# A WKV recurrence in chunks: numerators in two PSUM banks, state matmuls in the banks of the denominators, sums in 256 columns, v converted on the chip

## The chip, the cores and the metric

The kernel runs on one core of a Trainium2 chip. The metric is the time of one execution on the device, in microseconds (us). A core has five engines with in-order queues: PE (matmuls, with its weight loads shown apart as PEld), DVE (elementwise work), ACT (exponentials and logarithms), POOL and SP (here mostly issuers of DMAs). Matmul results go to PSUM, which has eight banks of 512 float32 columns in 128 partitions; everything else lives in SBUF. Transfers between device memory and SBUF are DMAs.

## What is computed

For each of 16 batches and 256 channels a recurrence runs over 2048 time steps. Without the running maximum `pp`, which only keeps the exponentials in range, it is a decayed sum of `exp(k)*v` over a decayed sum of `exp(k)`, with an extra weight `u` on the present step:

```python
for b in range(batch):                 # 16
    aa = bb = zeros(256); pp = full(256, -1e38)
    for t in range(seq_len):           # 2048
        kk, vv = k[b, t], v[b, t]
        ww = u + kk
        qq = maximum(pp, ww)
        e1, e2 = exp(pp - qq), exp(ww - qq)
        output[b, t] = (e1 * aa + e2 * vv) / (e1 * bb + e2 + 1e-08)
        ww = pp - w + kk
        qq = maximum(ww, kk)
        e1, e2 = exp(ww - qq), exp(kk - qq)
        aa, bb, pp = e1 * aa + e2 * vv, e1 * bb + e2, qq
```

k, v and the output are 33.6 MB each in float32.

## The kernel before

Time is cut into 16 chunks of 128 steps (two halves of 64), and the 16 batches into four groups of four. One pair of chunk c and group p is a slot, n = 4c + p, so there are 64 slots. A slot's tile has the 128 steps on the partitions and 4 batches x 256 channels = 1024 columns. A chunk is four slots.

In a slot n the main loop (L342) issues, for several slots at once:

- `load` (L62): the DMAs of k and v of slot n+6, on POOL's queue. For n of 8 and more and odd, `v_mode` (L59) says "dma", and the DMA converts v to bf16 on its way (`vb`, L70); otherwise v arrives as float32 (`vr`, L74) and DVE converts it (`cast_v`, L191).
- `round_k` (L161, DVE): k of slot n+2 is copied to a tile `km` in the matmul's float32 format.
- `logs` (L164, PE): eight matmuls make the exponents X of slot n+1 (decays from w and u, L170; k itself, L174) in four PSUM banks.
- `exps` (L178, ACT): exp of X of slot n, 2048 columns, into planes 0 and 1 of the ring EZR, which holds 12 slots. `times_v` (L196, DVE) multiplies them by v into planes 2 and 3.
- `den` (L296, PE): the denominators of slot q = n-9: four matmuls over planes 0 and 1 into two PSUM banks. `recip` (L302, L303, ACT): their reciprocals, by a logarithm and an exponential.
- `num` (L309, PE): half a numerator of slot qp = n-10: two matmuls over planes 2 and 3 into one PSUM bank. `mult` (L316, DVE): that half times the reciprocal, into the output tile. Both run twice a slot, and since there is one bank, the second `num` starts after the first `mult`. `store` (L321): the output's DMA, on POOL's queue.

The state at the end of a chunk has to reach all later chunks, and this is small work spread over the slots after the chunk's last one, s = 4c + 3:

- `sums` (L213, PE, slot s+1): 16 matmuls with 32 output rows, four beside each other in the array, sum the planes 0 and 2 of four slots over time, into one bank `tot` of 512 columns. `copy_sums` (L225, DVE) copies it to SBUF (`ts`).
- `turn` (L232, PE, s+2): matmuls that put the channels on the partitions (`TS`). `state_logs` (L237, ACT), `state_offsets` (L243 to L250, DVE): logarithms of the sums and the running offsets.
- `state_weights` (L254, ACT, s+3), `state_chain` (L261 to L268, DVE): the state itself; it reads TS again.
- `turn_back` (L275, PE, s+4): matmuls back to time order (`CT`). `inject` (L280, DVE): a copy to `cb`, and then four DMAs on SP's queue (L285) which patch one row of each half in the ring slots of the same chunk c with the state that enters it, before `den` (from slot 4c+9 on) and `num` read them.

`tot`, `TS` and `CT` share one PSUM bank of their own (pool `psm`). So the eight banks are X four, den two, num one, state work one. Every instruction keeps the order in which the program issues it on its engine (`K`). The list `later` (L324) says at which point of a slot a piece of state work is issued: "pe0", "act" and "dve0" come right after `exps`, before `num` and `den`; "pe" and "dve" come at the slot's end. So PE meets `turn` and `turn_back` at the head of a slot, before num and den of that slot.

The prediction names the lines of this kernel.

Of the kernel before, what the change touches and what calls it, by code (L numbers as in the profile page):

```python
# [7 lines left out]
F32 = mybir.dt.float32  # L8
F32R = mybir.dt.float32r
BF16 = mybir.dt.bfloat16  # L10
ALU = mybir.AluOpType
ACT = mybir.ActivationFunctionType
# [3 lines left out]
def kernel(  # L16
# [9 lines left out]
    K = tc.keep_in_program_order  # L26
    PE, DVE, SC, POOL, SP = nc.tensor, nc.vector, nc.scalar, nc.gpsimd, nc.sync

    B, T, Dm = k.shape
    HS = 64  # L30
# [18 lines left out]
    psx = ctx.enter_context(tc.tile_pool(name="psx", bufs=1, space=bass.MemoryType.PSUM))  # L49
    psd = ctx.enter_context(tc.tile_pool(name="psd", bufs=1, space=bass.MemoryType.PSUM))  # L50
    psn = ctx.enter_context(tc.tile_pool(name="psn", bufs=1, space=bass.MemoryType.PSUM))
    psm = ctx.enter_context(tc.tile_pool(name="psm", bufs=1, space=bass.MemoryType.PSUM))

    K(SC.preload_act_table_set("natural_log_exp_and_others"))

# [1 line left out]
    kr_of, vr_of, VB = {}, {}, {}  # L57

    def v_mode(n):  # L59
        return "dve" if n < 8 or n % 2 == 0 else "dma"  # L60

    def load(n, kq=None, vq=None):  # L62
        c, p = divmod(n, 4)
# [29 lines left out]
    def select(ap, cmp, fill, base, cm, pattern):  # L93
        K(POOL.affine_select(out=ap, in_=ap, pattern=pattern, compare_op=cmp,
                             fill=fill, base=base, channel_multiplier=cm))
# [4 lines left out]
    def fill(ap, value):  # L100
        K(DVE.memset(ap.bitcast(F32) if ap.dtype == F32R else ap, value))
# [1 line left out]
    select(M1, GE, 0.0, -1, -1, [[1, 128]])  # L103
    select(I1, NE, 1.0, 0, -1, [[1, 128]])
    COf = matrix("COf", F32)
    for h in range(2):
        K(POOL.iota(COf[HS * h:HS * h + HS, :], pattern=[[0, 2], [1, HS]], base=-HS // 2 - h, channel_multiplier=0,
                    allow_small_or_imprecise_dtypes=True))
    for g in (2, 3):
        select(COf, NE, 1.0, -32 * g - 1, 1, [[0, 128]])  # L110
# [15 lines left out]
    mats = {}  # L126

    def sum_matrices():
        OH = consts.tile([128, 40], BF16, tag="OH", name="OH")
        fill(OH, 0.0)  # L130
        for h in range(2):
            fill(OH[HS * h:HS * h + HS, 8 + h:9 + h], 1.0)
            fill(OH[HS * h:HS * h + 1, 16 + h:17 + h], 1.0)
        Sel = consts.tile([128, 3, 2, 4, 2], F32, tag="Sel", name="Sel")
        fill(Sel, 0.0)
        for j, r in ((0, 64), (1, 0), (2, 8)):
            select(Sel[:, j], NE, 1.0, -r, 1, [[-1, 2], [-2, 4], [-32, 2]])
        mats["OH"], mats["Sel"] = OH, Sel.rearrange("p a h c i -> p (a h) (c i)")

    def out_matrices():  # L140
        Lx = matrix("Lx", F32)
# [14 lines left out]
    def ez(n):  # L156
        return EZR[:, :, n % RING]

    def round_k(n):
        km = consts.tile([128, 4, Dm], F32R, tag=f"km{n % 2}", name="km") if n < 2 else KM[n - 2]  # L160
        K(DVE.tensor_copy(km, kr_of.pop(n)))  # L161
        KM[n] = km
# [37 lines left out]
    LL = consts.tile([128, 2, 2 * NST + 2, 32], F32, tag="LL", name="LL")  # L200
    A_of = [consts.tile([128, 8, 32], F32, tag=f"A{j}", name=f"A{j}") for j in range(2)]
    AB_of = [consts.tile([128, 2, 2, 32], F32, tag=f"AB{j}", name=f"AB{j}") for j in range(2)]

    CB_of = [consts.tile([128, 4, 128], BF16, tag=f"CB{j}", name=f"CB{j}") for j in range(2)]

    def state_start():
# [4 lines left out]
        K(DVE.memset(AB_of[0][:, :, 0, :], 0.0))  # L211

    def sums(c):  # L213
        t = psm.tile([128, D], F32, tag="misc", name="tot")
        for p in range(4):
            for j in range(4):
                q, i = divmod(j, 2)
                K(PE.matmul(t[32 * j:32 * j + 32, :], mats["OH"][:, 8 - 2 * p:40 - 2 * p],  # L218
                            ez(4 * c + p)[:, 2 * q, i, :], start=p == 0, stop=p == 3,
                            tile_position=(0, 32 * j), skip_group_check=True))  # L220
        st[c, "tot"] = t

    def copy_sums(c):
        ts = tiny.tile([128, D], F32, tag="ts", name="ts")
        K(DVE.tensor_copy(ts, st.pop((c, "tot"))))  # L225
        st[c, "ts"] = ts

    def turn(c):
        TS = psm.tile([128, 6, 4, 8], F32, tag="misc", name="TS")
        ts = st.pop((c, "ts"))  # L230
        for b in range(4):
            K(PE.matmul(TS[:, :, b, :], ts[:, 128 * b:128 * b + 128], mats["Sel"], start=True, stop=True,  # L232
                        skip_group_check=True))
        st[c, "TS"] = TS.rearrange("p a b m -> p a (b m)")

    def state_logs(c):
        K(SC.activation(LL[:, :, 2 * c + 2:2 * c + 4, :],  # L237
                        st[c, "TS"][:, 2:6, :].rearrange("p (a h) x -> p a h x", a=2), ACT.Ln))

    def state_offsets(c):  # L240
        A, last = A_of[c % 2], A_of[(c + 1) % 2]
# [13 lines left out]
        st[c, "G"] = G  # L255

    def state_chain(c):
        G, TS = st.pop((c, "G")), st.pop((c, "TS"))
        AB, nxt = AB_of[c % 2], AB_of[(c + 1) % 2]
        tb = tiny.tile([128, 2, 2, 32], F32, tag="tb", name="tb")  # L260
        K(DVE.tensor_mul(tb, TS[:, 0:4, :].rearrange("p (a h) x -> p a h x", a=2),  # L261
                         G[:, 4:6, :].unsqueeze(1).broadcast_to([128, 2, 2, 32])))
        for h in range(2):
            x = tiny.tile([128, 2, 32], F32, tag="x", name="x")
            K(DVE.tensor_mul(x, AB[:, :, h, :], G[:, h, :].unsqueeze(1).broadcast_to([128, 2, 32])))
            K(DVE.tensor_add(AB[:, :, 1, :] if h == 0 else nxt[:, :, 0, :], x, tb[:, :, h, :]))
        CB = CB_of[c % 2]
        K(DVE.tensor_mul(bass.AP(tensor=CB.tensor, offset=CB.offset, ap=[list(CB.ap[0]), [64, 2], [32, 2], [129, 4], [4, 8]]),  # L268
                         AB.rearrange("p a h (b m) -> p a h b m", b=4),
                         G[:, 2:4, :].rearrange("p h (b m) -> p h b m", b=4).unsqueeze(1).broadcast_to([128, 2, 2, 4, 8])))  # L270

    def turn_back(c):
        CT = psm.tile([128, 128], F32, tag="misc", name="CT")
        for b in range(4):
            K(PE.matmul(CT, CB_of[c % 2][:, b, :], mats["Id"], start=b == 0, stop=b == 3, skip_group_check=True))  # L275
        st[c, "CT"] = CT

    def inject(c):
        cb = small.tile([128, 128], BF16, tag="cb", name="cb")
        K(DVE.tensor_copy(cb, st.pop((c, "CT"))))  # L280
        r0 = 4 * c % RING
        for q in range(2):
            for h in range(2):
                r, x = HS * h + HS - 1, 32 * (2 * q + h)
                K(SP.dma_start(  # L285
                    out=EZR[r:r + 1, 2 * (1 - q), r0:r0 + 4, :, :].rearrange("o p i (b x) -> o (p i b) x", b=4),
                    in_=cb[x:x + 32, :]))
# [15 lines left out]
        K(SC.activation(rd, rd, ACT.Exp, scale=-1.0))  # L303
        RD[n] = rd

    def num(n, i):
        d = psn.tile([128, D], F32, tag="num", name="num")
        for m, q in (("LN", 2), ("IdN", 3)):
            K(PE.matmul(d, mats[m], ez(n)[:, q, i, :], start=q == 2, stop=q == 3, skip_group_check=True))  # L309
        NUM[n, i] = d  # L310

    def mult(n, i):
        if i == 0:
            OT[n] = opool.tile([128, 4, Dm], F32, tag="ot", name="ot")
        o = OT[n].rearrange("p (i n) d -> p i (n d)", i=2)
        K(DVE.tensor_mul(o[:, i, :], NUM.pop((n, i)), RD[n][:, i, :]))  # L316

    def store(n):
        RD.pop(n)
        c, p = divmod(n, 4)  # L320
        K(POOL.dma_start(out=out[4 * p:4 * p + 4, c * TC:(c + 1) * TC, :].rearrange("n t d -> t n d"),  # L321
                         in_=OT.pop(n)))

    later = {}  # L324
    for c in range(NST):
        s = 4 * c + 3
        for slot, where, f in ((s + 1, "pe", sums), (s + 1, "dve", copy_sums),
                               (s + 2, "pe0", turn), (s + 2, "act", state_logs), (s + 2, "dve", state_offsets),
                               (s + 3, "act", state_weights), (s + 3, "dve", state_chain),
                               (s + 4, "pe0", turn_back), (s + 4, "dve0", inject)):  # L330
            later.setdefault((slot, where), []).append((f, c))

    def small_work(n, where):
        for f, c in later.pop((n, where), []):
            f(c)
# [6 lines left out]
    for n in range(NP + LAG + 2):  # L342
        q, qp = n - LAG, n - LAG - 1
        live, out_q, out_qp = n < NP, 0 <= q < NP, 0 <= qp < NP
        if n + AHEAD < NP:
            load(n + AHEAD)
        if live:
            exps(n)
        small_work(n, "pe0")
        small_work(n, "act")  # L350
        small_work(n, "dve0")
        if out_qp:
            num(qp, 0)
        if out_q:
            den(q)
            recip(q)
        if out_qp:
            mult(qp, 0)
            num(qp, 1)
        if n + 1 < NP:  # L360
            logs(n + 1)
        if n + 2 < NP:
            round_k(n + 2)
        if out_qp:
            mult(qp, 1)
            store(qp)
        if live:
            times_v(n)
        if n + 1 < NP:
            cast_v(n + 1)  # L370
        if n == 1:
            sum_matrices()
        if n == 3:
            out_matrices()
        small_work(n, "pe")
        small_work(n, "dve")
    assert not later


# [29 lines left out]
```

## Time and profile before

| | |
|---|---|
| runs | 403.47, 408.91, 400.68 us; median 403.47 |
| profiled execution | 401.16 us, of which the recorded span is 399.2 |
| mean granted clock of PE in it | 0.923 of full |
| ACT: L178, L302, L303 | 64 each, mean 1875, 1019, 1061 ns |
| DVE: L196, L316 (512 columns), L161, L191 | 64, 128, 64, 36 of 1216, 690, 688, 698 ns |
| PE: L174, L296, L309 | 256, 254, 235 records |
| DMA from POOL's queue | 37824 packets, 91.24 MB, 78.2% of 16 engines' span |
| POOL issues: stores, k, v, v converted | 64, 62, 34, 28 |

The profiled execution is one run of the program on the chip with every instruction recorded. An engine's busy time is the sum of its instructions; idle time is put down to what released the instruction after it. A matmul's recorded end is modelled, and matmuls overlap, so their starts say more than their lengths. Some matmul records are missing (235 of 256 for L309).

### The profile page before, as it was taken

Reading aid. Unit: us, or ns where it says so; the run is one execution under the profiler, and the core shown is the slowest. Engines: PE = TensorE matmul, PEld = TensorE weight load, DVE = VectorE, ACT = ScalarE, POOL = GpSimd, SP = SyncE. Lnnn points to the kernel's source line nnn. Section 1 sums busy time; section 2 is a strip of 40 time slices with the busy share of each in tenths; the row PEclk is TensorE's granted clock in tenths of the full one; section 3 lists DMA queues with packets and bytes.
Section 4 is the critical chain, followed back from the end, with each engine's and each line's share of the span. In section 5 each row is a group of like instructions: output and inputs, shape, how many; then the busy total and the mean of one; then the engine's idle time right before and its main releaser. Section 6 shows DMA issues by size and latency. Waiting matters only on the chain.

```text
span 399.2 us, 4440 instructions
## 1 busy us (share of the span) xinstructions
PE 286.8 (72%) x1449; PEld 133.9 (34%) x1472; DVE 283.7 (71%) x559; ACT 260.6 (65%) x225; POOL 158.9 (40%) x203
## 2 busy tenths in 40 slices
PE   0345769787868697777789686869777778957672
PEld 0122334343424334333334242433433333423220
DVE  1266665877787877878777878787787977776542
ACT  1134344975777877877758777777787775876472
POOL 7134322452545453535435454545353531012131
PEclk9999857996999889999969999988999996999896
DMA  7978975699899989999989899997999991333344
GB/s 245 349 248 193 316 202 136 174 284 257 264 254 296 273 204 282 261 279 281 287 237 287 264 295 250 302 275 208 280 262 286 268 285 56 105 109 138 122 165 158
DMA packets 43062, 94.15 MB, mean 236 GB/s; under 512 B 6160, under 2 KB 22560, under 8 KB 43040
## 3 DMA queue, kind: packets, MB, share of 16 engines
q0 software_dynamic: 37824, 91.24, 78.2%
q1 hardware_dynamic: 4144, 1.59, 1.7%
q10 hardware_dynamic: 1072, 1.06, 0.9%
q8 instruction: 11, 0.18, 0.2%
q14 instruction: 11, 0.09, 0.1%
HBM read 67.13 MB, written 33.55 MB: 252 GB/s over the span
## 4 chain that ended last, share of the span: by engine, by line
PE 34%; DVE 29%; issue 21%; DMA 7%; ACT 4%; POOL 3%; POOLq 0%; DVEq 0%
DVE EZR L196 10%; PE num L309 10%; PE X L174 7%; DVE ot L316 7%; PE den L296 6%; DMA kr<-in_k_dram 4%; PE tot L218 3%; ACT EZR L178 3%; PE TS L232 3%; POOL out_dram L321 3%; DVE vb L191 3%; PE X L170 3%; DVE ts L225 2%; DMA out_dram<-ot 1%; DMA vr<-in_v_dram 1%
## 5 line engine op out<-in xcount | busy, mean ns | idle before, releaser
L178 ACT ACTIVATE EZR<-X 128x2048 bf16<-128x2048 f32 x64 | 120.0, 1875 | 51.7 <-PE X L174 51.4
L321 POOL DMA_DIRECT2D out_dram<-ot x64 | 48.9, 763 | 196.5 <-DVE ot L316 192.6
L316 DVE TENSOR_TENSOR ot<-num,rd 128x512 f32<-128x512 f32 x128 | 88.3, 690 | 53.7 <-PE num L309 44.5
L302 ACT ACTIVATE rd<-den 128x1024 f32<-128x1024 f32 x64 | 65.2, 1019 | 51.3 <-PE den L296 51.3
L196 DVE TENSOR_TENSOR EZR<-EZR,vb 128x2048 bf16<-128x2048 bf16 x64 | 77.8, 1216 | 5.4 <-ACT EZR L178 5.3
L309 PE MATMUL num<-EZR,LN 128*128 128x512 bf16 x121 | 49.0, 405 | 35.2 <-DVE ot L316 34.6
L303 ACT ACTIVATE rd<-rd 128x1024 f32<-128x1024 f32 x64 | 67.9, 1061 | 2.0
L66 POOL DMA_DIRECT2D kr<-in_k_dram x62 | 55.7, 899 | 16.9 <-DVE km L161 14.8
L170 PE MATMUL X<-WU,CO 1*128 1x512 f32 (+1 forms) x256 | 36.1, 554 | 27.9 <-ACT EZR L178 15.1
L174 PE MATMUL X<-km,NLE 128*128 128x512 f32 x128 | 51.9, 489 | 3.3 <-DVE km L161 3.3
L161 DVE CAST km<-kr 128x1024 fp32r<-128x1024 f32 x64 | 44.0, 688 | 8.6 <-DMA kr<-in_k_dram 6.1
L309 PE MATMUL num<-EZR,IdN 128*128 128x512 bf16 x114 | 46.3, 406 | 0.4
L174 PE MATMUL X<-km,NLZ 128*128 128x512 f32 x128 | 45.5, 440 | 0.0
L296 PE MATMUL den<-EZR,Id 128*128 128x512 bf16 x128 | 40.9, 403 | 0.1
L296 PE MATMUL den<-EZR,L 128*128 128x512 bf16 x126 | 40.4, 403 | 0.7
L170 PEld LDWEIGHTS X<-WU,CO 1*128 1x128 f32 (+1 forms) x256 | 13.5, 202 | 58.3 <-ACT EZR L178 26.5
L74 POOL DMA_DIRECT2D vr<-in_v_dram x34 | 31.0, 912 | 2.4 <-DVE vb L191 2.4
L309 PEld LDWEIGHTS <-IdN 128*128 128x128 bf16 x128 | 13.1, 102 | 54.7 <-issue 54.7
L174 PEld LDWEIGHTS X<-km,NLZ 128*128 128x128 f32 x128 | 27.0, 211 | 6.9
L174 PEld LDWEIGHTS X<-km,NLE 128*128 128x128 f32 x128 | 21.0, 207 | 21.5 <-issue 17.2
L232 PE MATMUL TS<-Sel,ts 128*128 128x48 f32 x128 | 17.4, 279 | 12.9 <-DVE ts L225 12.9
L275 PE MATMUL CT<-Id,CB 128*128 128x128 bf16 x64 | 7.6, 254 | 25.8 <-DVE CB L268 25.8
(53 smaller groups left out, 214.2 us busy)
## 6 DMA issues: line engine op xcount, KB each, us to landing
out_dram<-ot POOLq DMA_DIRECT2D x64, 512.0 KB, 4.1
kr<-in_k_dram POOLq DMA_DIRECT2D x62, 512.0 KB, 6.2
vr<-in_v_dram POOLq DMA_DIRECT2D x34, 512.0 KB, 6.6
vb<-in_v_dram POOLq DMA_DIRECT2D x28, 256.0 KB, 7.2
kr<-in_k_dram SPq DMA_DIRECT2D x2, 512.0 KB, 14.3
vr<-in_v_dram ACTq DMA_DIRECT2D x2, 512.0 KB, 5.7
EZR<-cb SPq DMA_DIRECT2D x64, 8.0 KB, 4.8
wuf<-in_w_dram SPq DMA_DIRECT2D x4, 2.0 KB
```

The lines of the kernel that those rows point to most:

```text
L66: K((kq or POOL).dma_start(out=kr, in_=src[0]))
L161: K(DVE.tensor_copy(km, kr_of.pop(n)))
L170: K(PE.matmul(X[:, q, i, :], CO[g:g + 1 + q, :], WU[g:g + 1 + q, :], start=True, stop=False, tile_position=(g, 0), skip_group_check=True))
L174: K(PE.matmul(X[:, q, i, :], m, km[:, i, :], start=False, stop=True, skip_group_check=True))
L178: K(SC.activation(ez(n)[:, 0:2], X_of.pop(n), ACT.Exp))
L196: K(DVE.tensor_mul(ez(n)[:, 2:4], ez(n)[:, 0:2], vb.unsqueeze(1).broadcast_to([128, 2, 2, D])))
L296: K(PE.matmul(d[:, i, :], mats[m], ez(n)[:, q, i, :], start=q == 0, stop=q == 1, skip_group_check=True))
L302: K(SC.activation(rd, DEN.pop(n), ACT.Ln, scale=RS))
L303: K(SC.activation(rd, rd, ACT.Exp, scale=-1.0))
L309: K(PE.matmul(d, mats[m], ez(n)[:, q, i, :], start=q == 2, stop=q == 3, skip_group_check=True))
L316: K(DVE.tensor_mul(o[:, i, :], NUM.pop((n, i)), RD[n][:, i, :]))
L321: K(POOL.dma_start(out=out[4 * p:4 * p + 4, c * TC:(c + 1) * TC, :].rearrange("n t d -> t n d"), in_=OT.pop(n)))
```

## The change

Six things are edited together.

1. `num` and `mult` work on a whole slot: four matmuls into two PSUM banks, and one DVE multiply of 1024 columns instead of two of 512.
2. The bank that this takes comes from state work: the pool `psm` is gone, and `tot`, `TS` and `CT` are allocated from `den`'s pool, which has one buffer. So they and the denominators follow one another in the same two banks.
3. `sums` writes 256 columns instead of 512: 32 matmuls of 256 columns, with the matrix OH shifted by 16 rows for the second half; the copy is half as wide, and `turn` takes two matmuls instead of four (with a wider Sel).
4. A new copy `copy_turned` (DVE) takes the 192 turned columns out of PSUM, and `state_logs` and `state_chain` read the copy.
5. `v_mode` always says "dve": no DMA converts, and DVE converts all of v.
6. The order: state work on PE comes last in its slot, behind `logs`, and its copies come last on DVE (a new point, "last"). `state_logs`, `state_offsets` and `state_weights` move to slot s+3 (the weights behind `recip`, "act2"), `state_chain` to the head of s+4 on DVE, with its small products in a new order, `turn_back` and `inject` to the end of s+4. `cast_v` comes before `mult`, and `times_v` after it.

```diff
     def v_mode(n):
-        return "dve" if n < 8 or n % 2 == 0 else "dma"
+        return "dve"
...
     def sums(c):
-        t = psm.tile([128, D], F32, tag="misc", name="tot")
+        t = psd.tile([128, 2, D], F32, tag="den", name="tot")
         for p in range(4):
-            for j in range(4):
-                q, i = divmod(j, 2)
-                K(PE.matmul(t[32 * j:32 * j + 32, :], mats["OH"][:, 8 - 2 * p:40 - 2 * p],
-                            ez(4 * c + p)[:, 2 * q, i, :], start=p == 0, stop=p == 3,
-                            tile_position=(0, 32 * j), skip_group_check=True))
+            for o in range(2):
+                x = 24 - 16 * o - 2 * p
+                for j in range(4):
+                    q, i = divmod(j, 2)
+                    K(PE.matmul(t[32 * j:32 * j + 32, 0, 0:Dm], mats["OH"][:, x:x + 32],
+                                ez(4 * c + p)[:, 2 * q, i, Dm * o:Dm * o + Dm],
+                                start=p == 0 and o == 0, stop=p == 3 and o == 1,
+                                tile_position=(0, 32 * j), skip_group_check=True))
         st[c, "tot"] = t
 
     def copy_sums(c):
-        ts = tiny.tile([128, D], F32, tag="ts", name="ts")
-        K(DVE.tensor_copy(ts, st.pop((c, "tot"))))
+        ts = tiny.tile([128, Dm], F32, tag="ts", name="ts")
+        K(DVE.tensor_copy(ts, st.pop((c, "tot"))[:, 0, 0:Dm]))
         st[c, "ts"] = ts
 
     def turn(c):
-        TS = psm.tile([128, 6, 4, 8], F32, tag="misc", name="TS")
+        t = psd.tile([128, 2, D], F32, tag="den", name="TS")
+        TS = t[:, 0, 0:192].rearrange("p (a n e m) -> p a n e m", a=6, n=2, e=2)
         ts = st.pop((c, "ts"))
-        for b in range(4):
-            K(PE.matmul(TS[:, :, b, :], ts[:, 128 * b:128 * b + 128], mats["Sel"], start=True, stop=True,
+        for e in range(2):
+            K(PE.matmul(TS[:, :, :, e, :], ts[:, 128 * e:128 * e + 128], mats["Sel"], start=True, stop=True,
                         skip_group_check=True))
-        st[c, "TS"] = TS.rearrange("p a b m -> p a (b m)")
+        st[c, "TS"] = t
+
+    def copy_turned(c):
+        T6 = small.tile([128, 6, 32], F32, tag="T6", name="T6")
+        K(DVE.tensor_copy(T6.rearrange("p a x -> p (a x)"), st.pop((c, "TS"))[:, 0, 0:192]))
+        st[c, "T6"] = T6
...
-    def num(n, i):
-        d = psn.tile([128, D], F32, tag="num", name="num")
+    def num(n):
+        d = psn.tile([128, 2, D], F32, tag="num", name="num")
         for m, q in (("LN", 2), ("IdN", 3)):
-            K(PE.matmul(d, mats[m], ez(n)[:, q, i, :], start=q == 2, stop=q == 3, skip_group_check=True))
-        NUM[n, i] = d
-
-    def mult(n, i):
-        if i == 0:
-            OT[n] = opool.tile([128, 4, Dm], F32, tag="ot", name="ot")
-        o = OT[n].rearrange("p (i n) d -> p i (n d)", i=2)
-        K(DVE.tensor_mul(o[:, i, :], NUM.pop((n, i)), RD[n][:, i, :]))
+            for i in range(2):
+                K(PE.matmul(d[:, i, :], mats[m], ez(n)[:, q, i, :], start=q == 2, stop=q == 3,
+                            skip_group_check=True))
+        NUM[n] = d
+
+    def mult(n):
+        OT[n] = opool.tile([128, 4, Dm], F32, tag="ot", name="ot")
+        K(DVE.tensor_mul(OT[n].rearrange("p (i n) d -> p i (n d)", i=2), NUM.pop(n), RD.pop(n)))
...
         s = 4 * c + 3
-        for slot, where, f in ((s + 1, "pe", sums), (s + 1, "dve", copy_sums),
-                               (s + 2, "pe0", turn), (s + 2, "act", state_logs), (s + 2, "dve", state_offsets),
-                               (s + 3, "act", state_weights), (s + 3, "dve", state_chain),
-                               (s + 4, "pe0", turn_back), (s + 4, "dve0", inject)):
+        for slot, where, f in ((s + 1, "pe", sums), (s + 1, "last", copy_sums),
+                               (s + 2, "pe", turn), (s + 2, "last", copy_turned),
+                               (s + 3, "act", state_logs), (s + 3, "dve", state_offsets),
+                               (s + 3, "act2", state_weights),
+                               (s + 4, "dve0", state_chain), (s + 4, "pe", turn_back),
+                               (s + 4, "last", inject)):
             later.setdefault((slot, where), []).append((f, c))
...
             exps(n)
-        small_work(n, "pe0")
         small_work(n, "act")
         small_work(n, "dve0")
-        if out_qp:
-            num(qp, 0)
         if out_q:
             den(q)
             recip(q)
         if out_qp:
-            mult(qp, 0)
-            num(qp, 1)
+            num(qp)
         if n + 1 < NP:
             logs(n + 1)
         if n + 2 < NP:
             round_k(n + 2)
+        if n + 1 < NP:
+            cast_v(n + 1)
         if out_qp:
-            mult(qp, 1)
+            mult(qp)
             store(qp)
+        small_work(n, "dve")
         if live:
             times_v(n)
-        if n + 1 < NP:
-            cast_v(n + 1)
         if n == 1:
             sum_matrices()
         if n == 3:
             out_matrices()
+        small_work(n, "act2")
         small_work(n, "pe")
-        small_work(n, "dve")
+        small_work(n, "last")
```

In the changed kernel a slot's order is thus, on PE: den(q), num(qp), logs(n+1), state work; on DVE: state_chain, round_k(n+2), cast_v(n+1), mult(qp), state_offsets, times_v(n), the copy of state work.

More of the change, by code (lines that the diff above doesn't have):

```diff
@@ L51 @@
     psn = ctx.enter_context(tc.tile_pool(name="psn", bufs=1, space=bass.MemoryType.PSUM))
-    psm = ctx.enter_context(tc.tile_pool(name="psm", bufs=1, space=bass.MemoryType.PSUM))
     K(SC.preload_act_table_set("natural_log_exp_and_others"))
@@ L105 @@
     COf = matrix("COf", F32)
-    for h in range(2):
-        K(POOL.iota(COf[HS * h:HS * h + HS, :], pattern=[[0, 2], [1, HS]], base=-HS // 2 - h, channel_multiplier=0,
+    for q in range(2):
+        K(POOL.iota(COf[64 * q:64 * q + 64, :], pattern=[[0, 2], [1, HS]], base=-HS // 2 - q, channel_multiplier=0,
                     allow_small_or_imprecise_dtypes=True))
@@ L128, in sum_matrices @@
     def sum_matrices():
-        OH = consts.tile([128, 40], BF16, tag="OH", name="OH")
+        OH = consts.tile([128, 56], BF16, tag="OH", name="OH")
         fill(OH, 0.0)
         for h in range(2):
-            fill(OH[HS * h:HS * h + HS, 8 + h:9 + h], 1.0)
-            fill(OH[HS * h:HS * h + 1, 16 + h:17 + h], 1.0)
-        Sel = consts.tile([128, 3, 2, 4, 2], F32, tag="Sel", name="Sel")
+            fill(OH[HS * h:HS * h + HS, 24 + h:25 + h], 1.0)
+            fill(OH[HS * h:HS * h + 1, 32 + h:33 + h], 1.0)
+        Sel = consts.tile([128, 3, 2, 2, 4, 2], F32, tag="Sel", name="Sel")
         fill(Sel, 0.0)
         for j, r in ((0, 64), (1, 0), (2, 8)):
-            select(Sel[:, j], NE, 1.0, -r, 1, [[-1, 2], [-2, 4], [-32, 2]])
-        mats["OH"], mats["Sel"] = OH, Sel.rearrange("p a h c i -> p (a h) (c i)")
+            for h in range(2):
+                select(Sel[:, j, h], NE, 1.0, -r - h, 1, [[-16, 2], [-2, 4], [-32, 2]])
+        mats["OH"], mats["Sel"] = OH, Sel.rearrange("p a h n c i -> p (a h) n (c i)")
     def out_matrices():
@@ L236, in state_logs @@
     def state_logs(c):
         K(SC.activation(LL[:, :, 2 * c + 2:2 * c + 4, :],
-                        st[c, "TS"][:, 2:6, :].rearrange("p (a h) x -> p a h x", a=2), ACT.Ln))
+                        st[c, "T6"][:, 2:6, :].rearrange("p (a h) x -> p a h x", a=2), ACT.Ln))
     def state_offsets(c):
@@ L257, in state_chain @@
     def state_chain(c):
-        G, TS = st.pop((c, "G")), st.pop((c, "TS"))
+        G, T6 = st.pop((c, "G")), st.pop((c, "T6"))
         AB, nxt = AB_of[c % 2], AB_of[(c + 1) % 2]
         tb = tiny.tile([128, 2, 2, 32], F32, tag="tb", name="tb")
-        K(DVE.tensor_mul(tb, TS[:, 0:4, :].rearrange("p (a h) x -> p a h x", a=2),
+        x, y = [tiny.tile([128, 2, 32], F32, tag=f"x{h}", name=f"x{h}") for h in range(2)]
+        K(DVE.tensor_mul(x, AB[:, :, 0, :], G[:, 0, :].unsqueeze(1).broadcast_to([128, 2, 32])))
+        K(DVE.tensor_mul(tb, T6[:, 0:4, :].rearrange("p (a h) x -> p a h x", a=2),
                          G[:, 4:6, :].unsqueeze(1).broadcast_to([128, 2, 2, 32])))
[L263 to L266, printed above, removed]
+        K(DVE.tensor_add(AB[:, :, 1, :], x, tb[:, :, 0, :]))
         CB = CB_of[c % 2]
@@ L270, in state_chain @@
                          G[:, 2:4, :].rearrange("p h (b m) -> p h b m", b=4).unsqueeze(1).broadcast_to([128, 2, 2, 4, 8])))
+        K(DVE.tensor_mul(y, AB[:, :, 1, :], G[:, 1, :].unsqueeze(1).broadcast_to([128, 2, 32])))
+        K(DVE.tensor_add(nxt[:, :, 0, :], y, tb[:, :, 1, :]))
     def turn_back(c):
-        CT = psm.tile([128, 128], F32, tag="misc", name="CT")
+        t = psd.tile([128, 2, D], F32, tag="den", name="CT")
         for b in range(4):
-            K(PE.matmul(CT, CB_of[c % 2][:, b, :], mats["Id"], start=b == 0, stop=b == 3, skip_group_check=True))
-        st[c, "CT"] = CT
+            K(PE.matmul(t[:, 0, 0:128], CB_of[c % 2][:, b, :], mats["Id"], start=b == 0, stop=b == 3,
+                        skip_group_check=True))
+        st[c, "CT"] = t
     def inject(c):
         cb = small.tile([128, 128], BF16, tag="cb", name="cb")
-        K(DVE.tensor_copy(cb, st.pop((c, "CT"))))
+        K(DVE.tensor_copy(cb, st.pop((c, "CT"))[:, 0, 0:128]))
         r0 = 4 * c % RING
@@ L304, in recip @@
         RD[n] = rd
-    def num(n, i):
-        d = psn.tile([128, D], F32, tag="num", name="num")
+    def num(n):
+        d = psn.tile([128, 2, D], F32, tag="num", name="num")
         for m, q in (("LN", 2), ("IdN", 3)):
-            K(PE.matmul(d, mats[m], ez(n)[:, q, i, :], start=q == 2, stop=q == 3, skip_group_check=True))
-        NUM[n, i] = d
-    def mult(n, i):
-        if i == 0:
-            OT[n] = opool.tile([128, 4, Dm], F32, tag="ot", name="ot")
-        o = OT[n].rearrange("p (i n) d -> p i (n d)", i=2)
-        K(DVE.tensor_mul(o[:, i, :], NUM.pop((n, i)), RD[n][:, i, :]))
+            for i in range(2):
+                K(PE.matmul(d[:, i, :], mats[m], ez(n)[:, q, i, :], start=q == 2, stop=q == 3,
+                            skip_group_check=True))
+        NUM[n] = d
+    def mult(n):
+        OT[n] = opool.tile([128, 4, Dm], F32, tag="ot", name="ot")
+        K(DVE.tensor_mul(OT[n].rearrange("p (i n) d -> p i (n d)", i=2), NUM.pop(n), RD.pop(n)))
     def store(n):
-        RD.pop(n)
         c, p = divmod(n, 4)
```

## The prediction

> **What bounds the kernel now.** I read the page first, then who waits for whom, then one chunk in order of time, then busy time chunk by chunk. A slot is one pass of the main loop (one n); a chunk is four slots, ending in state work. The page, engines first, then the PE clock and DMA in 40 slices, then the chain that ended last by engine:
>
> ```profile
> PE 286.8 (72%) x1449; PEld 133.9 (34%) x1472; DVE 283.7 (71%) x559; ACT 260.6 (65%) x225; POOL 158.9 (40%) x203
> ...
> PEclk9999857996999889999969999988999996999896
> DMA  7978975699899989999989899997999991333344
> ...
> PE 34%; DVE 29%; issue 21%; DMA 7%; ACT 4%; POOL 3%; POOLq 0%; DVEq 0%
> ```
>
> No engine is full, and the chain alternates between PE and DVE: this is a kernel of handovers. DMA looks near its limit, so I asked who waits for a load. Columns: us in total, times, longest us.
>
> ```profile
> ACT rd L302 <- PE den L296: 51.3, 36, 4.3
> DVE ot L316 <- PE num L309: 44.5, 46, 1.8
> PE num L309 <- DVE ot L316: 34.6, 33, 1.8
> ...
> PE CT L275 <- DVE CB L268: 25.8, 16, 2.2
> ...
> DVE km L161 <- DMA kr<-in_k_dram: 6.1, 1, 6.1
> ```
>
> One wait for a load, in the ramp. The other rows are PE and DVE passing single PSUM buffers back and forth (num/ot), and PE standing still in front of state work (CT), with den, which ScalarE needs, queued behind. Order of time, the costliest slot of a chunk (start, us, engine, line; in brackets the idle time before and who ended it):
>
> ```profile
> 188.11 0.38 PE L309 MATMUL num<-EZR,LN 128*128 128x512 bf16 x1 [0.35 <-DVE ot L316]
> ...
> 190.21 1.05 PE L218 MATMUL tot<-EZR,OH 128*32 128x512 bf16 x16
> ...
> 191.31 0.69 DVE L225 COPY ts<-tot 128x512 f32<-128x512 f32 x1 [0.75 <-PE tot L218]
> 192.06 0.97 PEld L232 LDWEIGHTS TS<-Sel,ts 128*128 128x128 f32 x8 [1.29 <-DVE ts L225]
> 192.06 1.09 PE L232 MATMUL TS<-Sel,ts 128*128 128x48 f32 x8 [0.80 <-DVE ts L225]
> ...
> 193.42 0.59 PE L296 MATMUL den<-EZR,L 128*128 128x512 bf16 x2
> ...
> 194.48 1.02 ACT L302 ACTIVATE rd<-den 128x1024 f32<-128x1024 f32 x1 [1.02 <-PE den L296]
> ```
>
> Sums, copy, turn, num, den, and only then ScalarE: this slot lasts 6.3 us between starts of L178, the four of a chunk 3.8, 6.3, 5.2-5.5 and 5.7. Three chunks whole (stretch, length, then busy us of PE, PEld, DVE, ACT, POOL, clock, DMA share, GB/s):
>
> ```profile
> 186.50:209.50 23.00, 18.52 (x92) 8.36 (x92) 17.45 (x34) 16.21 (x14) 10.40 (x14) 0.85 0.93 260
> 209.50:230.30 20.80, 16.22 (x91) 7.73 (x92) 16.98 (x33) 16.16 (x15) 9.94 (x12) 1.00 0.94 271
> 230.30:251.30 21.00, 16.22 (x92) 7.74 (x93) 17.25 (x34) 16.23 (x15) 10.19 (x13) 1.00 0.96 279
> ```
>
> A chunk takes 21.0 us, or 23.0 when a stretch at half PE clock falls in it (every third).
>
> **The change, part by part.** I lay the new order onto one chunk, for DVE and PE, from these rows: L161 and L191 0.61 us from start to start back to back (186.76 to 187.37), L196 1.14-1.2, den plus num eight matmuls 0.215 apart, so 1.95 from the release to the last end; from that release to X ready (L170/L174 behind them) 3.5; handovers 0.05.
>
> *One multiply of 1024 columns (L316).* 0.69 for 512 columns; 128x128 PSUM reads (L280) take 0.29, so 0.4/384 columns, about 0.16 fixed. I take 1.22, 1.14 to the next start. Ends: 1.07 (no fixed part beyond the streaming) and 1.38 (two old ones). PE no longer stands between two nums.
>
> *Every v converted on DVE.* Two more L191 a chunk, 2 x 0.61. Off the path goes: L70's loads. In the trace's DMA records they are 512 packets of 62 ns (1.98 us of 16 engines) against 128 packets of about 199 ns (1.59). DMA falls from 19.9 to 19.1 us a chunk: it was not waited for, so nothing is gained; if the cover of six-ahead loads went, 19.1 would still lie under 21. POOL issues as many DMAs as before and mostly waits for ot (192.6 us).
>
> *Sums in 256 columns.* 32 pairs instead of 16, half as long. Individual records of L218 start in groups of four, 0.216 us apart, which is the streaming; L275's pairs of 128 columns follow each other in 0.056. Eight groups of 0.108 give 1.05 again. Ends: 1.0 and 32 x 0.056 + 0.2 = 2.0 if the column groups stop overlapping. I take 1.05, as L218 is the same operation. [...] The copy ts shrinks to 0.42 (0.16 + 256 columns).
>
> *State matmuls in den's banks.* The heart of it. den of slot n+1 now waits until DVE has copied tot, TS or CT, each the last thing on DVE in its slot; behind den, PE queues num and the next X, and DVE's multiply waits for num. By slot, from the copy that ends the one before (s=4c+3):
> - s+1 (sums): PE leads. X ready 3.5, sums end 4.65, copy to 5.15.
> - s+2 (turn): DVE has L161 and L191 (1.24), waits for num to 2.04, multiply to 3.2, L196 to 4.4, copy of the 192 turned columns (0.36): 4.75. The turn itself (8 parts in 1.09, now 4 of double width, 0.7-0.8) ends at 4.3, hidden.
> - s+3: num 2.04, multiply 3.2, state_offsets 1.41 (L243-L250 now) 4.6, L196 5.7. G waits at ScalarE for the offsets, to 5.0; the next L178 starts then, not at 3.5, but DVE needs it only at 9.6.
> - s+4: state_chain (L261-L268) 1.55, L161, L191, multiply, L196, copy cb: DVE without a gap, 5.4, to 11.1.
> Together 21.0: exactly the chunk of before. PE's stops in front of TS, CT and num go (73 us of waits), and three waits of about 0.8 for num plus the PE-led slot come in.
>
> *The patch (inject) is later.* Its copy moves from early in slot s+4 to that slot's end; the four SP DMAs behind it feed the den two slots on, which is one slot of cover less. In the loaded part of the run their last packets land 4.3 to 6.4 us after the copy's end (13 chunks, median 5.1); den wants them at 5.2. Averaged over those 13: 0.25 a chunk.
>
> So +0.3 a chunk, 13 chunks: **+4**. Ends: 0 (all landed, sums 1.0) and +13 (sums 2.0, or landings 1 us later).
>
> *Half-clock stretches.* Each costs 2.0 now, since PE is on the path nearly everywhere. In the new order PE leads 8.5 of 21 us, so 6.8 us at half speed cost about 1.4; four in the steady part: **-3**. Ends -8 (none occur) and +5 (more occur, since PE's pauses move).
>
> *The tail.* From the end of the last L196 (360.0) to the end, 39.2 us. New: slots 64 to 69 carry the last state work and patch (about 22 us by the same sums), then four slots of num 1.03 and multiply 1.22 handing one buffer back and forth, 2.3 each (2.9 now), then 5.1 of store: 36.4. **-3**, ends -6 and +1. The ramp (4.8 a slot, exps and X in turn) I leave: state work there has no den beside it.
>
> Sum: the profiled execution took 401.16 (span 399.2 and 2.0 around it); 401.16 + 4 - 3 - 3 = 399.2. It lies 0.57% below the median of the runs, 403.47; on that scale **401.5**.
>
> **Rivals.** *The clock stays up (faster).* For: the waits that go are PE pauses of up to 2.2 us, which may be what lets the clock fall. Against: new pauses of the same size come before den in s+1 and after s+4's X. Price: -8.4 for the four stretches instead of -3, patches in time +0.7 instead of +4: 401.16 - 8.4 + 0.7 - 3 = 390.5, or 392.7 on the median's scale.
>
> *The patch lands late (slower).* At the first den of a chunk PE stands, and num, X, DVE's multiply stand behind it. Every us of landing beyond 5.2 after the copy costs a us a chunk. For: 3 of 13 landings now exceed 5.8. Against: DMA carries fewer packets. At 6.4 each time it is +1.2 x 13 instead of +3: 411.5 on the span's scale, 414 on the median's; it decides from a mean of about 6.2.
>
> *The sums really take 2.0.* The PE-led slot grows by 0.95: +12, so 413.5. For: twice the pairs; against: L218's starts.
>
> *It does not shorten the multiply* (1.38): on DVE in three of four slots, 0.16 x 39: +6, still no change.
>
> **How the numbers follow.** Forecast 0.47, clock 0.23, late patch 0.15, long sums 0.11, others slower 0.04. Two per cent (8 us) is about what a measurement of this kernel, whose runs spread from 400.7 to 408.9, can tell from no change. Faster 0.24, the same 0.47, slower 0.29. Range 392 to 415: from the clock rival's time to that of the late patch; the forecast's own terms, clock and patch as taken, give 394 (no 0.3 a chunk, tail -6) to 411 (multiply of 1.38, tail +1).
>
> **What would show it.** Right: a chunk without half clock near 21.3 us; den waiting for DVE's ts, T6 and cb copies three times a chunk; ot waiting for num about 0.8; L70 and its 512-byte packets gone with no load waited for; tail slots of 2.3. Sums far from 1.05, den waiting on the patch over 0.5 a chunk, or clock stretches more or fewer than five make terms wrong; DVE idle inside slots s+3 and s+4 would make the layout itself wrong.

## The result and the profile after

| | median (lowest to highest) | ratio to the kernel before, 95% interval |
|---|---|---|
| before, in the same comparison | 402.14 us (400.68 to 408.91) | 1 |
| after | 431.43 us (426.61 to 435.78) | 1.068 [1.058, 1.078] |

The change makes the kernel 6.8% slower; 431 lies above the range. The profiled execution took 435.78 us (span 433.7). It is the longest of the four; between starts of L178, two of its chunks took 26.7 and 27.5 us, and the others 22.6 to 25.2.

From the page of after: engines, PE clock and DMA in 40 slices, and the row of the new multiply.

```profile
PE 300.8 (69%) x1634; PEld 147.0 (34%) x1664; DVE 295.9 (68%) x539; ACT 259.5 (60%) x225; POOL 154.1 (36%) x206
...
PEclk9999999596879889596969989667886969698987
DMA  8978874878687889888787886867888885232445
...
L326 DVE TENSOR_TENSOR ot<-num,rd 128x1024 f32<-128x1024 f32 x64 | 78.3, 1223 | 82.9 <-ACT rd L312 47.6
```

The multiply is what was forecast, 1223 ns, and the waits of PE and DVE for one another over num and ot, 79 us before, are 8 now. But DMA, which was mostly at 9 before, is mostly at 8 or lower, and the clock line dips all along. Who waits for whom now (us in total, times, longest us):

```profile
DVE ot L326 <- ACT rd L312: 47.6, 19, 5.2
...
ACT rd L312 <- PE den L306: 40.5, 29, 2.8
...
PE den L306 <- DVE cb L290: 26.9, 15, 2.2
PE den L306 <- DMA EZR<-cb: 22.3, 11, 3.7
...
```

Two rows are news. `den` waits for the patch's DMAs, 22.3 us in eleven waits; the prediction had 0.25 us a chunk, some 3 us in all. And it waits up to 2.2 us for the copy `cb`, PE standing still meanwhile. Three chunks, one after the other (stretch, length, busy us of PE, PEld, DVE, ACT and POOL, clock, DMA share, GB/s):

```profile
149.50:173.30 23.80, 17.96 (x108) 8.74 (x109) 19.26 (x34) 17.01 (x16) 9.66 (x12) 0.86 0.85 278
173.30:196.90 23.60, 18.68 (x101) 9.20 (x103) 17.47 (x33) 15.51 (x14) 9.53 (x12) 0.79 0.82 259
196.90:221.30 24.40, 17.39 (x105) 8.42 (x105) 18.91 (x34) 16.26 (x16) 9.84 (x12) 0.85 0.82 260
```

The chunk was forecast at 21.3 us. It is about 24, and every one of the three is below full clock, where before two of three were at 1.00. By the clock records, half clock came in stretches of mostly 6.8 us about every third chunk before (34 us in the 12 chunks from slot 12 on), and comes in every one of these chunks now, in stretches of mostly 6.8 or 10.2 us (104 us). The end of one chunk and the start of the next, in order of time; the next is one of the two long ones (start, us, engine, line; in brackets the idle time before and who ended it):

```profile
247.93 0.28 DVE L290 CAST cb<-CT 128x128 bf16<-128x128 f32 x1
...
248.24 3.12 SPq L295 DMA_DIRECT2D EZR<-cb  x4
248.26 0.58 PE L306 MATMUL den<-EZR,L 128*128 128x512 bf16 x1 [2.15 <-DVE cb L290]
...
253.10 1.06 PE L219 MATMUL tot<-EZR,OH 128*32 128x256 bf16 x32
...
254.21 0.42 DVE L227 COPY ts<-tot 128x256 f32<-128x256 f32 x1
...
257.82 0.78 PE L306 MATMUL den<-EZR,L 128*128 128x512 bf16 x2 [3.66 <-DMA EZR<-cb]
...
259.49 1.02 ACT L312 ACTIVATE rd<-den 128x1024 f32<-128x1024 f32 x1 [4.41 <-remote]
```

The copy `cb` ends at 248.21 and the four patch DMAs are issued. The sums, here at full clock, take 1.06 us and `ts` is out of the shared banks at 254.63; by the prediction's layout `den` starts then. It starts at 257.82, 9.6 us after the copy, and behind it wait num, X and ScalarE. The prediction let the patch in at 5.2. The 3.2 us from `ts` to `den` here are the most of any chunk; over the 13 chunks with loads in flight the wait past `ts` is 1.25 on average.

From the start of L178 in slot 12 to its start in slot 60 (12 chunks): 261.2 us before, 295.8 after, so 21.8 and 24.7 a chunk. The difference of 34.6 is as much as the span grew (34.5). The tail is 39.0 (39.2 before). So only the chunk is to be explained: the late patch, the half clock, or the shared banks themselves.

### The profile page after: what moved, and what is told of

Read it like the earlier page. It is cut to its first block, busy times and chain, and to the rows that moved or that the text cites. A ratio compares the mean times of both kernels' runs of the same rounds, so it can differ in the third digit from the quotient of the medians.

```text
span 433.7 us, 4726 instructions
## 1 busy us (share of the span) xinstructions
PE 300.8 (69%) x1634; PEld 147.0 (34%) x1664; DVE 295.9 (68%) x539; ACT 259.5 (60%) x225; POOL 154.1 (36%) x206
## 3 DMA queue, kind: packets, MB, share of 16 engines
q10 hardware_dynamic: 1072, 1.06, 0.8%
## 5 line engine op out<-in xcount | busy, mean ns | idle before, releaser
L178 ACT ACTIVATE EZR<-X 128x2048 bf16<-128x2048 f32 x64 | 119.7, 1870 | 69.2 <-PE X L174 69.1
L326 DVE TENSOR_TENSOR ot<-num,rd 128x1024 f32<-128x1024 f32 x64 | 78.3, 1223 | 82.9 <-ACT rd L312 47.6
L312 ACT ACTIVATE rd<-den 128x1024 f32<-128x1024 f32 x64 | 65.4, 1022 | 70.9 <-PE den L306 40.5
L65 POOL DMA_DIRECT2D kr<-in_k_dram x62 | 53.2, 858 | 12.2 <-DVE km L161 10.0
L174 PE MATMUL X<-km,NLE 128*128 128x512 f32 x128 | 54.9, 515 | 2.6 <-DVE km L161 2.6
L73 POOL DMA_DIRECT2D vr<-in_v_dram x62 | 49.8, 804 | 19.4 <-DVE vb L191 17.2
L161 DVE CAST km<-kr 128x1024 fp32r<-128x1024 f32 x64 | 47.1, 738 | 8.3 <-DMA kr<-in_k_dram 5.3
L191 DVE CAST vb<-vr 128x1024 bf16<-128x1024 f32 x64 | 50.2, 784 | 0.0
L174 PE MATMUL X<-km,NLZ 128*128 128x512 f32 x128 | 48.5, 466 | 0.0
L320 PE MATMUL num<-EZR,LN 128*128 128x512 bf16 x127 | 45.2, 441 | 3.0 <-DVE ot L326 1.9
L306 PEld LDWEIGHTS <-L 128*128 128x128 bf16 x128 | 11.6, 105 | 78.9 <-issue 54.7
L320 PEld LDWEIGHTS <-LN 128*128 128x128 bf16 x128 | 14.2, 111 | 23.5 <-issue 13.0
```

The source lines that it names most:

```text
L65: K((kq or POOL).dma_start(out=kr, in_=src[0]))
L174: K(PE.matmul(X[:, q, i, :], m, km[:, i, :], start=False, stop=True, skip_group_check=True))
L178: K(SC.activation(ez(n)[:, 0:2], X_of.pop(n), ACT.Exp))
L191: K(DVE.tensor_copy(vb, vr))
L306: K(PE.matmul(d[:, i, :], mats[m], ez(n)[:, q, i, :], start=q == 0, stop=q == 1, skip_group_check=True))
L312: K(SC.activation(rd, DEN.pop(n), ACT.Ln, scale=RS))
```

## The experiments

Each was timed in three rounds beside the kernel before, whose medians in these comparisons lie between 402.7 and 405.4 us. Ratios are to that.

**e1_lag10: the patch gets a slot more.** The changed kernel, with the denominators one slot later.

```diff
-    LAG = 9
+    LAG = 10
```

> The changed kernel with LAG 10 instead of 9, so den and num of a slot come one slot later and the patch has one slot more of cover; nothing else differs, the tail is one slot longer (about 2.5 us). Late-patch theory: no den waits for the patch, chunks of 21.0 to 21.5 us where the clock is full, half-clock stretches as rare as before the change, 400 to 406 us in all. Shared-bank theory (den behind DVE's copies of tot, TS and CT makes PE pause, and the pauses bring the half clock): still over 420 us, half-clock stretches in every chunk.

425.62 us, 1.048 [1.041, 1.056]. `den` waits for no patch any more, and the kernel is hardly faster. The end of one of its chunks and the start of the next in order of time, and the row of the first:

```profile
238.28 0.51 PE L170 MATMUL X<-WU,CO 1*128 1x512 f32 x4 [1.64 <-ACT EZR L178]
...
239.75 0.40 PE L284 MATMUL CT<-Id,CB 128*128 128x128 bf16 x4
...
242.30 0.59 PE L306 MATMUL den<-EZR,L 128*128 128x512 bf16 x1 [2.15 <-DVE cb L290]
...
243.10 1.06 PE L306 MATMUL den<-EZR,Id 128*128 128x512 bf16 x2 [0.22 <-issue]
```

```profile
218.50:242.70 24.20, 18.84 (x103) 9.14 (x104) 18.06 (x32) 16.07 (x14) 9.34 (x13) 0.78 0.81 262
```

PE pauses 1.64 us before X and 2.15 us before `den`, and at once two matmuls of 512 columns take 1.06 us, where a pair takes 0.59 at full clock: half clock, here in the slot in which PE leads. That slot, which starts the chunk, is 8.5 us from L178 to L178 instead of 5.7. The patch alone is not the answer; the pause at the shared banks looks like the other half.

**e3_before_late_patch: the late place alone.** The kernel before, with only `turn_back` and `inject` moved to the slot's end. Converting loads, one numerator bank and the state's own bank stay.

```diff
-                               (s + 4, "pe0", turn_back), (s + 4, "dve0", inject)):
+                               (s + 4, "pe", turn_back), (s + 4, "dve", inject)):
```

> The kernel before, with turn_back and inject alone moved to the end of slot s+4 as in the change (own bank for state work, half numerators, converting loads and 512-column sums kept). Late-patch theory: den waits for the patch once a chunk, 1 to 4 us each, 412 to 432 us. Shared-bank theory: within 1% of 402, as no bank is shared; a little faster is possible since PE no longer stands in front of CT.

425.62 us, 1.049 [1.042, 1.055], as the late-patch theory expected. From its waits:

```profile
ACT rd L302 <- PE den L296: 63.9, 27, 5.8
...
PE den L296 <- DMA EZR<-cb: 30.1, 13, 3.7
```

The last packet of the patch, measured from the end of the copy, over the 13 chunks with loads in flight (worked out from the DMA records):

| | median | longest |
|---|---|---|
| before | 5.1 | 6.4 |
| e3, before with the late place | 7.4 | 9.2 |
| after | 7.8 | 8.6 |
| after with LAG 10 (e1) | 6.7 | 7.9 |

So the place in the slot makes the patch 2 to 3 us later, in the kernel before as in the changed one. Converting loads are not what decides it: e3 has them and lands late, and e11 below has none, keeps the early place, and lands at 4.5 (median; 5.2 at most). `den` starts another 0.7 to 1.2 us after the last packet, where it is the patch that it waited for. Neither was in the prediction. Why the four DMAs take longer in this place is not settled. In e3 the queues move 2.4 to 2.7 MB in the 8 us after the copy, before 1.4 to 2.0; but in after it is only 2.0 to 2.2, with the longest landings. Nor is e3's loss the wait alone: half clock falls in 11 of its 12 chunks (65 us, against 34 before), and its one chunk without it takes 21.9.

**e5_lag10_fill: the pauses filled.** e1, with spare matmuls where PE stands: seven after `turn_back`, into the second bank of its tile which nothing reads, and the denominators issued in slot s+4 computed twice.

```diff
+        for _ in range(7):
+            K(PE.matmul(t[:, 1, :], mats["Id"], ez(4 * c + 3)[:, 0, 0, :], start=True, stop=True,
+                        skip_group_check=True))
...
-            den(q)
+            den(q, 2 if n % 4 == 3 else 1)
```

> E1's kernel (LAG 10) with PE kept busy in slot s+4: seven matmuls of 512 columns behind turn_back into the second bank of CT's tile, which nobody reads, and den of that slot made twice over. Clock theory (E1's 24.2 us chunk is 21 us plus one half-clock stretch, let in by PE's pauses of 1.6 and 2.2 us in slot s+4): the stretch goes from most chunks, the slot after goes from 8.5 to 5.2-5.4 us, chunks 21.0 to 21.5, 392 to 405 us in all, although PE does about 3 us more work a chunk. Rival, that the slot with the sums is as long as that for its own sake (bank handover, sums): 424 to 430 us.

385.93 us, 0.954 [0.946, 0.961]. More work, 40 us less. Two chunks:

```profile
200.70:221.20 20.50, 17.73 (x115) 8.99 (x115) 18.26 (x34) 16.07 (x14) 10.18 (x13) 1.00 0.91 308
221.20:241.70 20.50, 17.74 (x115) 9.07 (x115) 18.45 (x34) 16.07 (x14) 9.62 (x13) 1.00 0.94 310
```

Clock 1.00, and 20.5 us in each of the 12 chunks. Sharing the banks costs nothing beyond what was in the layout (21.0).

**e8_fill_lag9: the fill without the extra slot.** The changed kernel (`LAG = 9`) with e5's fill.

> The changed kernel (LAG 9) with E5's filling of PE's pauses in slot s+4: the second half of the pair E1/E5. The two causes as substitutes (a half-clock stretch makes the slot with the sums 3 us longer, and the patch lands meanwhile; without the stretch den stands and waits for the patch): no stretch in that slot, den waits about 3.3 us a chunk for the patch (landing 7 to 8 after the copy, 0.9 to be seen, against 5.0), chunks of 23.5 to 24, 420 to 432 us, hardly better than the change itself. If the clock alone were the cause: 384 to 392, as E5.

458.55 us, 1.130 [1.120, 1.140]: worse than after, and both expectations missed. From its waits, and from its timeline:

```profile
ACT rd L315 <- PE den L309: 97.7, 45, 6.0
...
PE den L309 <- DMA EZR<-cb: 51.1, 14, 5.0
```

```profile
251.84 1.01 PE L309 MATMUL den<-EZR,L 128*128 128x512 bf16 x2 [3.25 <-DMA EZR<-cb]
252.65 1.06 PE L309 MATMUL den<-EZR,Id 128*128 128x512 bf16 x2
```

With the clock full, the slot of the sums is short and `den` comes to the patch earlier: it waits 3.2 us a chunk on average past `ts` (1.25 in after). That wait is itself a pause of PE (3.25 us here), and the matmuls after it are at half clock: 1.01 and 1.06 us for two, against 0.59 at full clock. In after, a half-clock stretch in the sums' slot had been covering part of the landing: in the four chunks where that slot lasts 8.5 us, `den` waits at most 0.6 past `ts`, in the others up to 3.2; in e8 the slot is 5.6 to 5.9 each time.

**e12_fill_patch_aside: is it the patch?** e8, with the four DMAs writing to a tile that nobody reads; so it leaves out the state that later steps need, and only its time counts. The DMAs have as many packets of the same size.

```diff
-                K(SP.dma_start(
-                    out=EZR[r:r + 1, 2 * (1 - q), r0:r0 + 4, :, :].rearrange("o p i (b x) -> o (p i b) x", b=4),
-                    in_=cb[x:x + 32, :]))
+                K(SP.dma_start(out=aside[x:x + 32, :], in_=cb[x:x + 32, :]))
```

> E8's kernel (the change, LAG 9, PE's pauses in slot s+4 filled) with the four patch DMAs of a chunk writing to a tile of their own that nobody reads; the state does not reach the following steps' outputs. Same LAG as the change, so it tells whether E5's gain over E8 is the patch or something else that LAG 10 brings. Patch theory: no wait, chunks of 20.5, 381 to 387 us. If LAG 10 helped in another way: 400 or more.

381.26 us, 0.942 [0.933, 0.951], as the patch theory expected; all 12 chunks 20.5, and no half clock before the tail. One of them:

```profile
136.50:157.00 20.50, 17.79 (x119) 9.01 (x117) 18.48 (x33) 16.11 (x15) 9.63 (x12) 1.00 0.93 306
```

The last packets land as late as in after (median 7.8), but nothing waits for them. So what made e8 slow is the wait for the patch, and not something else that LAG 10 brings. The tail is 37.4 us here and 41.5 in e5, which has one slot more to drain. The changed kernel with the patch aside and its pauses left open was not measured.

**e7_before_late_lag10 and e10_before_late_lag10_fill: what the rest of the change brings.** e3 with LAG 10; and that with a small fill (the denominators issued in slot s+3 computed twice).

```diff
-    LAG = 9
+    LAG = 10
...
-            den(q)
+            den(q, 2 if n % 4 == 2 else 1)
```

> E3's kernel (before, with turn_back and inject alone late) with LAG 10. Late-patch theory: the wait for the patch goes, and with it E3's loss: 401 to 408 us. If moving turn_back and inject behind the slot's other work costs for another reason: 418 to 428.

> E7's kernel with den of slot s+3 made twice over, to fill PE's pause of 1.75 us there. E7 had a half-clock stretch of 3.4 us in every chunk, and chunks of 20.5. This is E5's counterpart with the parts of the kernel before (half numerators, state work in a bank of its own, converting loads, sums of 512 columns), both without wait for the patch and with a full clock, and so the price of the change's other parts. If these parts together bring nothing: 384 to 388 us, as E5. If state work in den's banks costs more than the parts save, as E6 and E9 say: chunks of 18.8 to 20, 362 to 378. If they save: over 390.

e7: 382.28 us, 0.944 [0.935, 0.952], far below what was expected. Once the patch has its cover, moving `turn_back` and `inject` late gains some 20 us, and the 25.8 us for which PE stood before CT are not among its waits any more. LAG 10 without the move was not measured; in the kernel before, nothing waits for the patch that it would cover. Every chunk has a half-clock stretch of 3.4 us and still lasts 20.5. e10: 381.41 us, 0.944 [0.934, 0.954]; one chunk:

```profile
204.20:224.20 20.00, 16.94 (x97) 8.11 (x97) 17.00 (x34) 16.17 (x14) 9.68 (x13) 1.00 0.99 285
```

20.0 us at full clock, with one numerator bank, half multiplies and converting loads: 0.5 less than the change with the same cover. This fell between the expectations. The two banks, the long multiply and the rest, taken together, bring nothing while state work sits in the banks of the denominators.

**e11_before_all_dve: v converted on DVE, alone.**

```diff
-        return "dve" if n < 8 or n % 2 == 0 else "dma"
+        return "dve"
```

> The kernel before with v_mode always dve, the one part of the change that is separate from the banks and the order. By the prediction's sum two more conversions of 0.61 us a chunk lie on DVE, which is idle 4 us a chunk: between 0 and 1.2 us a chunk, 402 to 417 us; if the converting loads held anything up (DMA share 0.93 to 0.97), faster, 390 to 400.

420.85 us, 1.044 [1.035, 1.052], above what was expected. At full clock its chunk takes 21.2, some 0.3 more for the added DVE work, but ten of 12 chunks take 23 to 24. PE's pause before CT is longer:

```profile
212.31 0.40 PE L275 MATMUL CT<-Id,CB 128*128 128x128 bf16 x4 [2.44 <-DVE CB L268]
```

and half clock falls in those ten (68 us in all, against 34 in these 12 chunks before). The prediction costed this edit by its work and by the loads. That its price is the longer pause fits these rows but is not shown: no run of e11 has its pauses filled, and none has the changed kernel with converting loads.

**e6_state_in_num_banks and e9_num_banks_fill: state work in the other two banks.** e1, with `tot`, `TS` and `CT` in the numerators' banks, so that `den`, which ScalarE needs first, goes ahead of the wait; the rows that `den` reads are patched first. e9 adds a fill: the denominators issued in slot s+4 computed three times.

```diff
-        t = psd.tile([128, 2, D], F32, tag="den", name="tot")
+        t = psn.tile([128, 2, D], F32, tag="num", name="tot")
...
-        for q in range(2):
+        for q in (1, 0):
...
-            den(q)
+            den(q, 3 if n % 4 == 3 else 1)
```

> E1's kernel with tot, TS and CT in the banks of the numerators instead of the denominators, and the two patch DMAs that den needs issued first. Shared-bank theory: den and ScalarE no longer wait for DVE's last copy, num does, and num (0.9 us to its last start) lies beside the two conversions at the head of DVE's slot; three waits of 0.8 us of DVE and 0.9 us of the PE-led slot go, a chunk of 18.6 to 19.5 us with a full clock, 370 to 388 us; with a half-clock stretch in every chunk still, 400 to 412. If only the clock counts and the bank does not: 420 to 428.

> E6's kernel with den of slot s+4 made three times over, to fill PE's pause of 2 us there; nothing else. E6 had chunks of 18.6 to 18.8 with a full clock and 21.3 with a half-clock stretch, in two of three chunks. Clock theory: most stretches go, chunks of 18.6 to 19.3 (DVE busy 18.3, DMA 19.1 at the packet times of before), 350 to 364 us. If the pause that lets the clock fall is another one: 372 to 380.

Both came out as the shared-bank and clock theories expected. e6: 376.52 us, 0.928 [0.919, 0.937]; chunks (here between starts of L312) of 18.6 to 18.8 at full clock, and of 20.0 to 22.7, two of three, where a half-clock stretch costs time. e9: 357.50 us, 0.884 [0.878, 0.891]; two chunks:

```profile
226.60:245.20 18.60, 17.11 (x113) 8.62 (x113) 18.30 (x33) 15.96 (x15) 9.61 (x13) 1.00 0.96 333
245.20:263.80 18.60, 17.28 (x113) 8.62 (x113) 18.28 (x33) 15.94 (x15) 9.58 (x13) 1.00 0.98 340
```

18.3 of 18.6 us are DVE's: the kernel is now bound by one engine, with DMA close behind. This is the fastest version, 11.6% below the kernel before.

The four corners of the main question, in us and in us per chunk:

| | PE's pauses left | pauses filled |
|---|---|---|
| LAG 9 | 431.4 (22.6 to 25.2, two of 27) | 458.6 (24.2 to 28.0) |
| LAG 10 | 425.6 (mostly 24.2) | 385.9 (20.5) |

Neither cure works alone. A sum of two terms would not show this.

## Why the prediction was wrong, point by point

- *The layout of a chunk* held: 21.0 forecast, 20.5 in e5 and e12, where clock and patch are out of the way. So did the multiply (1.22; 1223 ns), `ts` (0.42; 424 ns) and `copy_turned` (0.36; 0.35). *Sums* of 1.05 measured 1.06 at full clock. The *turn* was 0.58 (0.7 to 0.8 forecast). No load was waited for after the ramp, and the 512-byte packets are gone.
- *"Averaged over those 13: 0.25 a chunk"* failed: the patch. The prediction moved the four DMAs and kept their landing times from the old place. They came at 7.8 (median) instead of 5.1, and `den` starts up to 1.2 us after that. At the prediction's own price, a us for each us beyond 5.2, these landings are 2.4 a chunk. The wait past `ts` is 1.25 a chunk in after, and 3.2 where the clock doesn't hide it (e8). The rival *the patch lands late* was one half of the mechanism, with a bound (6.4 at most) taken from the place that the change left.
- *"Half-clock stretches ... -3"* failed, and in sign. It kept the number of stretches and made each cheaper (four at 0.6 less are 2.4, rounded up), with a few more of them only in its upper end of +5. They came in every chunk, longer, and in the very slot in which PE leads. A chunk with half clock in it (mean clock 0.78) and without a wait for the patch is 24.2 (e1), against 20.5 at clock 1.00 (e5): 3.7 us a chunk. The text had the fact in hand ("new pauses of the same size come before den in s+1 and after s+4's X"), but used it only against the rival in which the clock stays up. A rival of its own, a stretch in every chunk, was missing. With the 2.8 us by which a stretch lengthens the PE-led slot (8.5 in e1, 5.7 in e5) it gives 21.3 + 2.8 = 24.1, about the measured chunk; that 2.8 was known only afterwards.
- *Together*: a chunk of 24.2 on average, leaving out the two of 27, is 20.5 and 3.7 for patch and clock. How much belongs to which has no answer, as the table shows: the stretch hides a part of the landing, and the wait for the patch brings half clock of its own (e8).
- *The tail*: 36.4 forecast, 39.0 measured. Its slots are 2.40 (2.3); without the wait for the patch and with the pauses filled it is 37.4 (e12).

## What to carry to other kernels

A DMA that was moved within this loop didn't take its landing time along (5.1 us in before, 7.4 in e3, 7.8 in after): measure it anew in the new place, and count what passes between its last packet and the instruction that waits (0.7 to 1.2 us here). Where PE's clock drops in the profile of before, ask of each edit which pauses of PE it lengthens, shortens or puts close together, and in which slot the half clock would then fall; here half clock over a slot that PE leads cost 3.7 us a chunk (e1, clock 0.78 in the chunk shown, against e5, 1.00), and a stretch of 3.4 us elsewhere 0.5 (e7 has one in each chunk and takes 20.5, e10 has none and takes 20.0). Before judging a design, take one cover more and fill the pauses: here that turned a 6.8% loss into a gain of 4.6%. Only then did it pay to ask where the small work should sit: in the other pair of banks, with the same cover and a fill of its own, the gain is 11.6% (e9).

## What the runs showed of the hardware

- *Half clock without a long pause.* By the clock records five half-clock stretches begin in the 12 chunks of before from slot 12 on, each 6.8 us long, and fifteen in those of after, two of 3.4 us, nine of 6.8 and four of 10.2. In the 3.4 us ahead of each of before's five, PE's matmuls were busy for 1.64 to 1.84 us, and the longest pause of PE was 1.8 us. They were busy for as little, 1.63 to 1.80 us, with pauses as long, in the 3.4 us from 116.0, 180.9, 245.8 and 310.6 us of before, and no drop followed. What makes the difference, no run shows. In e1 the pauses ahead of the half-clock matmuls at 243.1 us were 1.64 and 2.15 us.
- *About one stretch a chunk.* In after, stretches begin 23.9 us apart from 77 us to 221 and from 299 to 371, where chunks average 24.1 and 24.0. e7 has one of 3.4 us in every chunk of 20.5. Whether the loop sets this period or the clock does, no run shows.
- *Spare matmuls can pay.* In e5 PE does more, and the kernel takes 40 us less than e1; in e9 19 less than e6. In e8 the same fill as e5's, without the extra slot, cost 27 (458.6 against 431.4).
